# Second conditioning columns on ScalarE, output matrix at unit 13, state outputs and scores in pairs of 64 rows

## The chip, the core and the metric

The kernel runs on one core of one Trainium2 chip. The core has five engines that run side by side: TensorE (PE in the profile, its weight loads PEld), VectorE (DVE), ScalarE (ACT), GpSimd (POOL) and SyncE (SP, which here only issues transfers and takes branches). Each works through its own queue in order, and they wait for each other by semaphores. The metric is the device time of one execution in microseconds (us), lower is better.

## The reference

One layer of a diffusion backbone with 512 latent tokens and 256 context tokens of 1024 channels, all float32, cut to what matters here:

```python
mod = silu(c) @ ada_w + ada_b;  mod_c = silu(c_ctx) @ ada_w + ada_b
sh1, sc1, g1, sh2, sc2, g2 = split(mod, 6);  csh1, csc1, ... = split(mod_c, 6)
h  = rms_norm(x, norm_mix_w) * (1 + sc1) + sh1          # latent
hc = rms_norm(ctx, norm_mix_w) * (1 + csc1) + csh1      # context
p, pc = h @ w_in, hc @ w_in                             # q, k, v, r, low rank, u
gla = gated linear attention of q, k, v in chunks, both directions, times silu(r)
s5  = complex diagonal state space over u, both directions, then gelu and GLU
x = x + g1 * (concat([gla, s5]) @ w_out)
h2 = rms_norm(x, norm_ffn_w) * (1 + sc2) + sh2
x = x + g2 * moe(h2)             # the top 4 of 32 experts, clamped SwiGLU
return rms_norm(x, final_norm_w)
```

## The kernel before

The **prologue** (0 to about 480 us of the profile) computes everything up to the routing of h2. The **expert loop** after it streams the weights of all 32 experts (1 MB pieces gu and dn) and multiplies the tokens that were routed to each. The prologue is put in order by a scheduler, from the order of the code and priorities (`high_priority` moves work ahead), with stretches whose order on some engines is written by hand (`manual_schedule`).

**First stage.** The projection to u, the S5 inputs, is done in 32 units: four parts h of the 1024 input channels (256 each), times four 128-column tiles of the latent (`pu`, 512 columns wide) and of the context (`puc`, 256 wide). On TensorE and ScalarE their order is the loop `for i, (h, o)` (i from 4 to 31), into which other work is put at certain numbers i:

- `ADA1 = (7, 8, 9, 10)`: the shifts of the second half of the conditioning (`ps_ada`, L273). After the last, `columns(1)` makes the scale A1 and the shift B1 of channels 512 to 1023 for latent and context: the rows are copied from PSUM to `mrow` (L282), turned by two transposes into `ps_mod` (L115), and added to and multiplied by weight columns. Then `modulate(1)` (L555) applies them in eight activations to xn and xc. Parts h = 2 and 3 (units 16 to 31) need it.
- `LOW = 20`: the low rank gates. `OUT = 23`: `output_columns` turns the S5 output matrix in two runs of 32 small transposes (`ps_c`, L441), each copied to `cc` by ScalarE (L443). From `COND0 = 12` each unit also does a piece of the other conditioning product (`pa`, L527), whose weights `adb` come through SyncE. From `CHUNK0 = 14` each unit turns four blocks of chunk weights (`ps_w`), which VectorE makes at L428 to L430 (`wr`, `wi`, with `wtmp`) and ScalarE copies to `wt` (L422).

`work(...)` gives a buffer from one ring of four (tag t2k) that mrow, wtmp, bt, uT and others share. After unit 31 ScalarE copies pu to `uT`, SyncE sends it out (`ud`), and VectorE makes the products `cl` (L467 to L469, with wtmp again). Then TensorE computes q, k (`pk`), v and r, while VectorE scans the S5 states (`XV`) up to about 304 us.

**Second stage** (304 to 363 us). `space_out(j)` makes the S5 outputs py: for each of 16 pairs of groups, two products of `TZ` with U (64 columns each) and four of `xb` with cl. xb holds the states of two groups of 64 rows as block diagonals (128x128, zeros elsewhere), copied out of XV by ScalarE (first group, L997) and VectorE (second, L995). `attend(tp)` does the linear attention of two chunks: for each of two heads h2 of a pair (rows 0 to 63, rows 64 to 127) four score products `psc` (64 rows, L1047), masked into `pm_` by ScalarE and VectorE (L1052 to L1055), four products of states `po<-sm` (L1060) and two of values (L1062). A float32 product is two records in the profile.

**The join.** `gla_out` normalizes po to gl, whose transposes pgl start behind a branch on SyncE (`steep`, L1086); the output projection pmx follows. SyncE's queue ahead of that branch holds loads of x, `wo` and the first `gu`.

## Time and profile before

| | |
|---|---|
| time before, median of 3 runs | 1516.83 us (1516.59 to 1519.24) |
| the profiled execution | 1516.56 us |
| its span in the profile | 1514.7 us |
| TensorE busy over the span | 1345.6 us (89%) |
| VectorE, ScalarE, GpSimd busy | 529.8, 251.1 and 178.1 us |
| bytes moved by DMA | 487.19 MB, mean 322 GB/s |

The page of the profile divides the span into 40 slices and gives for each the busy share of every engine and of the 16 DMA engines. Other views give the busy time in a stretch, or an engine's instructions in the order of time: start, duration, line, operation, what is written from what, shapes, count, and in brackets the idle time ahead of it and what ended that. One line can stand for several records ("x4"), whose duration then runs from the first start to the last end. PEclk is the share of full speed (2.4 GHz) that TensorE's clock was granted.

### The profile page before, as it was taken

Reading aid. Unit: us, or ns where it says so; the run is one execution under the profiler, and the core shown is the slowest. Engines: PE = TensorE matmul, PEld = TensorE weight load, DVE = VectorE, ACT = ScalarE, POOL = GpSimd, SP = SyncE. Lnnn points to the kernel's source line nnn. Section 1 sums busy time; section 2 is a strip of 40 time slices with the busy share of each in tenths; the row PEclk is TensorE's granted clock in tenths of the full one; section 3 lists DMA queues with packets and bytes.
Section 4 is the critical chain, followed back from the end, with each engine's and each line's share of the span. In section 5 each row is a group of like instructions: output and inputs, shape, how many; then the busy total and the mean of one; then the engine's idle time right before and its main releaser. Section 6 shows DMA issues by size and latency. Waiting matters only on the chain. (4 is left out here: it accounts for less than half of the span.)

```text
span 1514.7 us, 21032 instructions
## 1 busy us (share of the span) xinstructions
PE 1345.6 (89%) x8123; PEld 544.4 (36%) x8123; DVE 529.8 (35%) x1373; ACT 251.1 (17%) x552; POOL 178.1 (12%) x158
## 2 busy tenths in 40 slices
PE   5679689997997899999998999999998988788985
PEld 2334354476443233333333333333332223222322
DVE  5941848966155221321122211222211132112125
ACT  4122351163121100100001000010000010000014
POOL 1030000000002010120102011111111111111110
PEclk9889799998997999999999999999999999999998
DMA  9565225134466999999999999999999999999993
GB/s 327 187 213 177 72 84 125 42 123 174 167 218 230 391 370 415 409 408 412 413 413 407 418 406 412 413 413 410 412 407 405 412 414 410 408 407 409 411 406 117
DMA packets 108428, 487.19 MB, mean 322 GB/s; under 512 B 25470, under 2 KB 32398, under 8 KB 59152
## 3 DMA queue, kind: packets, MB, share of 16 engines
q1 hardware_dynamic: 92704, 457.16, 75.8%
q0 software_dynamic: 13872, 24.72, 6.0%
q10 hardware_dynamic: 1728, 3.56, 0.6%
q8 instruction: 88, 1.44, 0.4%
q14 instruction: 36, 0.29, 0.1%
HBM read 468.41 MB, written 22.86 MB: 324 GB/s over the span
## 5 line engine op out<-in xcount | busy, mean ns | idle before, releaser
L1637 PE MATMUL pg<-gu,xT 128*64 128x512 f32 x2048 | 480.3, 601 | 35.2 <-DMA gu<-in_exp_w_gu_dram 28.6
L1637 PEld LDWEIGHTS pg<-gu,xT 128*64 128x64 f32 x2048 | 138.1, 137 | 331.4 <-issue 240.9
L1670 PE MATMUL pd<-dn,aT 128*64 128x512 f32 x992 | 222.8, 594 | 12.2 <-DMA dn<-in_exp_w_down_dram 9.6
L1657 DVE TENSOR_SCALAR at<-rest 128x256 f32<-128x256 f32 x32 | 13.6, 425 | 544.6 <-PE rest L1650 307.8
L1658 ACT ACTIVATE sgm<-at 128x256 f32<-128x256 f32 x96 | 39.7, 414 | 699.2 <-DVE at L1657 658.8
L1670 PEld LDWEIGHTS pd<-dn,aT 128*64 128x64 f32 x992 | 68.4, 136 | 145.8 <-issue 110.6
L1605 POOL DMA_INDIRECT xg<-h2d,iu x47 | 50.3, 1069 | 590.9 <-DVE li L1659 297.3
L1650 PE MATMUL rest<-gu,xT 128*32 128x512 f32 x896 | 107.3, 597 | 0.0
L1721 POOL DMA_INDIRECT acc<-y,iu x30 | 47.1, 1569 | 195.0 <-DMA acc<-yr,iu 165.7
L1621 ACT ACTIVATE aT<-turn 128x512 f32<-128x512 f32 x64 | 27.9, 487 | 204.8 <-PE turn L115 199.9
L1721 POOL DMA_INDIRECT acc<-yr,iu x30 | 48.1, 1604 | 63.1 <-DMA acc<-y,iu 40.0
L1719 DVE SCALAR_TENSOR_TENSOR yr<-rest,gt,g2r 128x256 f32<-128x256 f32 x30 | 14.5, 483 | 104.2 <-DMA acc<-yr,iu 71.6
L1680 PE MATMUL rest<-dn,aT 128*32 128x256 f32 x896 | 50.8, 379 | 0.0
L1650 PEld LDWEIGHTS rest<-gu,xT 128*32 128x32 f32 x896 | 24.4, 109 | 69.1 <-issue 67.9
L115 PE MATMUL turn<-ident,at 128*128 128x128 f32 x192 | 31.9, 302 | 9.4 <-PEq L1755 4.7
L1519 DVE CAST e<-mt 96x64 bf16<-96x64 f32 x32 | 6.1, 200 | 90.8 <-PEq L1755 46.8
L1661 DVE TENSOR_TENSOR at<-at,sgm 128x256 f32<-128x256 f32 x96 | 37.6, 419 | 0.0
L1660 DVE SCALAR_TENSOR_TENSOR at<-li,at 128x256 f32<-128x256 f32 x96 | 37.5, 418 | 0.0
L577 PE MATMUL pu<-xn,wu_w 128*128 128x512 f32 x64 | 35.7, 686 | 1.2 <-issue 1.2
L115 PEld LDWEIGHTS turn<-ident,at 128*128 128x128 f32 x192 | 25.8, 209 | 30.2 <-issue 25.9
L1567 DVE TENSOR_TENSOR ohs<-mt 128x1024 bf16<-128x1024 f32 x30 | 36.5, 1216 | 0.0
L115 PE MATMUL turn<-ident,xg 128*128 128x128 f32 x192 | 28.1, 284 | 6.9 <-PEq L1746 5.5
(554 smaller groups left out, 1434.2 us busy)
## 6 DMA issues: line engine op xcount, KB each, us to landing
gu<-in_exp_w_gu_dram SPq DMA_DIRECT2D x252, 1024.0 KB
dn<-in_exp_w_down_dram SPq DMA_DIRECT2D x128, 1024.0 KB
adb<-in_ada_w_dram SPq DMA_DIRECT2D x32, 512.0 KB
ada<-in_ada_w_dram SPq DMA_DIRECT2D x16, 512.0 KB
wo<-in_w_out_dram SPq DMA_DIRECT2D x4, 1024.0 KB
gu<-in_exp_w_gu_dram POOLq DMA_DIRECT2D x4, 1024.0 KB, 8.4
xt<-in_x_dram SPq DMA_DIRECT2D x4, 512.0 KB
wu_w<-in_w_in_dram SPq DMA_DIRECT2D x4, 512.0 KB
```

The lines of the kernel that those rows point to most:

```text
L115: nc.tensor.transpose(ps, src, ident[:k, :k])
L577: nc.tensor.matmul(o, lhs(k, w[:, kk]), rhs(k, w[:, kk]), start=opens and k == 0, stop=k == KT - 1, skip_group_check=True)
L1567: V.tensor_tensor(ohs, iot.rearrange("p (o s) r -> p o (s r)", o=1).to_broadcast([P, 4, 2 * P]), pm.to_broadcast([P, 4, 2 * P]), op=OP.is_ ...
L1605: last = nc.gpsimd.indirect_dma_start(out=x[:, c0:c1], out_offset=None, in_=src, in_offset=bass.IndirectOffsetOnAxis(ap=iu[:, s:s + 1], ax ...
L1637: nc.tensor.matmul(pg[b][64 * q:64 * q + 64], xT[:, k % 4, (k // 4) * 64:(k // 4 + 1) * 64], gu[k][:, :, c:c + 256], start=False, stop=(k ...
L1650: nc.tensor.matmul(pr[32 * q:32 * q + 32], xT[:, 4 + k % 2, (k // 2) * 32:(k // 2 + 1) * 32], gu[k][:, :, q * 256:(q + 1) * 256], start=Fa ...
L1658: nc.scalar.activation(sg, at, AF.Sigmoid, scale=1.702)
L1660: V.scalar_tensor_tensor(at, li, 1.0, at, op0=OP.add, op1=OP.mult)
L1661: V.tensor_tensor(at, at, sg, op=OP.mult)
L1670: nc.tensor.matmul(pd[64 * q:64 * q + 64], aT[:, k % 4, (k // 4) * 64:(k // 4 + 1) * 64], dn[k][:, q * 512:(q + 1) * 512], start=False, st ...
L1680: nc.tensor.matmul(pe[32 * q:32 * q + 32, 0:256], aT[:, 4 + k % 2, (k // 2) * 32:(k // 2 + 1) * 32], dn[k][:, q * 256:(q + 1) * 256], star ...
L1721: nc.gpsimd.indirect_dma_start(out=dst, out_offset=bass.IndirectOffsetOnAxis(ap=iu[:, s:s + 1], axis=0), in_=src, in_offset=None, bounds_c ...
```

## The change

It has six parts. (1) `mrow` of the second conditioning half gets a buffer of its own. (2) Its A1 and B1 are made by eight ScalarE activations of 128x2 straight from PSUM, with bias and scale from columns; the copy `pms` and the six GpSimd operations go. `one_more` now holds (1 + b) w. The first half stays on VectorE. (3) `OUT` goes from 23 to 13, `COND0` from 12 to 11 and `CHUNK0` from 14 to 12. (4) Two edge fills of kc2 move from VectorE to GpSimd. (5) `space_out` reads the states from XV: each block diagonal product becomes two of 64 rows and 64 columns, one per group, next to each other, on rows and columns 0 to 63 and 64 to 127. xb, its copies and its zero fills go. (6) `attend` issues the score products and the products of states of both heads in turn, ahead of the masks; each head has its own PSUM bank for scores.

```diff
-OUT = 23
-COND0 = 12
-CHUNK0 = 14
+OUT = 13
+COND0 = 11
+CHUNK0 = 12
...
-            mrow = work("mrow", (P, 256))
+            mrow = consts.tile([P, 256], F32, name="mrow1") if p else work("mrow", (P, 256))
...
-            if p:
-                pms = consts.tile([P, 256], F32, name="pms")
-                nc.scalar.activation(pms, pm[:, :256], AF.Copy)
-                pm = pms
...
+            if p:
+                for kk in range(4):
+                    a, b, w = [o[:, n + 4 * p + kk:n + 4 * p + kk + 1] for o, n in ((one_more, 0), (cols, 16), (cols, 32))]
+                    nc.scalar.activation(A1[p][:, :, kk], pmv[:, 1, kk // 2, kk % 2, 0:2], AF.Identity, bias=a, scale=w)
+                    nc.scalar.activation(B1[p][:, :, kk], pmv[:, 0, kk // 2, kk % 2, 0:2], AF.Identity, bias=b)
+                return
...
-                eng.tensor_tensor(a_, pmv[:, 1, :, :, j], one_more[:, p].rearrange("p (h b) -> p h b", h=2), op=OP.add)
-                eng.tensor_tensor(a_, a_, col(32), op=OP.mult)
-                eng.tensor_tensor(b_, pmv[:, 0, :, :, j], col(16), op=OP.add)
+                V.scalar_tensor_tensor(a_, pmv[:, 1, :, :, j], 1.0, col(24), op0=OP.add, op1=OP.add)
+                V.tensor_tensor(a_, a_, col(32), op=OP.mult)
+                V.tensor_tensor(b_, pmv[:, 0, :, :, j], col(16), op=OP.add)
...
-    V.memset(kc2[:, 0, :, LC - 1:LC], 0.0)
-    V.memset(kc2[:, 1, :, 0:1], 0.0)
+    nc.gpsimd.memset(kc2[:, 0, :, LC - 1:LC], 0.0)
+    nc.gpsimd.memset(kc2[:, 1, :, 0:1], 0.0)
...
-                        nc.tensor.matmul(o, x[:, i % 2, d * 2 + r].rearrange("p g w -> p (g w)"),
-                                         cl[j][r][:, d, gl_].rearrange("p k c -> p (k c)"),
-                                         start=False, stop=(d == 1 and r == 1), skip_group_check=True)
+                        for g2 in range(2):
+                            xh = XV[g2 * 64:(g2 + 1) * 64]
+                            src = bass.AP(tensor=xh.tensor, offset=xh.offset + gp * 260 + d * 131 + r * 65,
+                                          ap=[list(xh.ap[0]), [1, 64]])
+                            nc.tensor.matmul(o[g2 * 64:(g2 + 1) * 64], src,
+                                             cl[j][r][g2 * 64:(g2 + 1) * 64, d, gl_].rearrange("p k c -> p (k c)"),
+                                             start=False, stop=(d == 1 and r == 1), skip_group_check=True)
...
+            pb = [bank("psc").rearrange("p (z h t) -> p z h t", z=2, h=2) for h2 in range(2)]
...
+            for z in range(2):
+                for hp in range(2):
+                    for h2 in range(2):
+                        nc.tensor.matmul(pb[h2][:, z, hp], kd[z][hs[h2], hp, c * P:(c + 1) * P],
+                                         qd[z][hs[h2], hp, c * P:(c + 1) * P], start=True, stop=True)
```

What the scheduler makes of it is shown at three places. First TensorE behind the second conditioning half, before (`ps_ada` are the shifts, `wu_w` the weights of the units, `adb` those of the conditioning):

```order
L273 MATMUL ps_ada_604<-ada_157,stc 32x256 x8
L115 MATMUL ps_mod<-ident,mrow 128x128 x2
L577 MATMUL puc_197<-xc,wu_w_146 128x256 x2
L577 MATMUL pu_195<-xn_108,wu_w_146 128x512 x2
L527 MATMUL pa_735<-adb_199,stc 32x512 x4
L577 MATMUL puc_198<-xc,wu_w_146 128x256 x2
L527 MATMUL pa_735<-adb_199,stc 32x512 x4
L577 MATMUL pu_196<-xn_108,wu_w_146 128x512 x2
```

and after:

```order
L273 MATMUL ps_ada_604<-ada_157,stc 32x256 x8
L115 MATMUL ps_mod<-ident,mrow_645 128x128 x2
L578 MATMUL puc_197<-xc,wu_w_146 128x256 x2
L528 MATMUL pa_733<-adb_199,stc 32x512 x4
L578 MATMUL pu_195<-xn_108,wu_w_146 128x512 x2
L528 MATMUL pa_733<-adb_199,stc 32x512 x4
L115 MATMUL ps_w<-ident,wr_558 128x128 x4
L578 MATMUL puc_198<-xc,wu_w_146 128x256 x2
L442 MATMUL ps_c_756<-ident,crow_105 64x32 x32
L442 MATMUL ps_c_790<-ident,crow_106 64x32 x32
```

The first chunk weights (ps_w) now stand two units earlier, and the output matrix (ps_c) ten. On ScalarE at the same place before:

```order
L282 ACTIVATE mrow<-ps_ada_604 128x256
L290 ACTIVATE pms<-ps_mod 128x256
L555 ACTIVATE xn_109<-xn_109,B_653,A_652 128x512
L555 ACTIVATE xc<-xc,B_653,A_652 128x256
L555 ACTIVATE xn_109<-xn_109,B_653,A_652 128x512
```

and after (A and B are the scale and shift columns):

```order
L281 ACTIVATE mrow_645<-ps_ada_604 128x256
L293 ACTIVATE A_650<-ps_mod,one_more,cols 128x2
L294 ACTIVATE B_651<-ps_mod,cols 128x2
L293 ACTIVATE A_650<-ps_mod,one_more,cols 128x2
L294 ACTIVATE B_651<-ps_mod,cols 128x2
```

Two more pairs of A and B follow there before the modulations, which are the same eight. The third place is TensorE at the first state outputs, before (pst, pkt and pp belong to the attention states):

```order
L999 MATMUL py<-TZ_1859,U_1074 64x128
L999 MATMUL py<-TZ_1859,U_1075 64x128
L999 MATMUL py<-TZ_1859,U_1074 64x128
L999 MATMUL py<-TZ_1859,U_1075 64x128
L936 MATMUL pst<-vc,kt__2017 64x128 x8
L115 MATMUL pkt_2051<-ident,cum_1269 128x128 x4
```

and after:

```order
L983 MATMUL py<-TZ_1859,U_1074 64x128
L983 MATMUL py<-TZ_1859,U_1075 64x128
L992 MATMUL py<-cl_1110,XV 64x128 x2
L992 MATMUL py<-cl_1111,XV 64x128 x2
L992 MATMUL py<-cl_1110,XV 64x128 x2
L992 MATMUL py<-cl_1111,XV 64x128 x2
L983 MATMUL py<-TZ_1859,U_1074 64x128
L983 MATMUL py<-TZ_1859,U_1075 64x128
L992 MATMUL py<-cl_1110,XV 64x128 x2
L992 MATMUL py<-cl_1111,XV 64x128
L937 MATMUL pst<-vc,kt__2017 64x128 x16
L115 MATMUL pkt_2051<-ident,cum_1269 128x128 x4
```

The products with cl no longer wait for copies of XV and stand ahead of the attention states; each x2 is a pair of row halves.

## Rows read from the trace of the kernel before

**Rows 1.** the page's forty slices: busy tenths of the DMA engines

```profile
DMA  9565225134466999999999999999999999999993
```

**Rows 2.** busy time by stretch: columns engine busy (instructions), PEclk, DMA share, GB/s

```profile
70.00:80.00 10.00, 2.56 (x7) 2.17 (x8) 10.00 (x18) 0.77 (x2) 1.37 (x1) 0.50 0.00 2
130.00:140.00 10.00, 10.00 (x58) 4.33 (x56) 3.06 (x5) 2.39 (x4) 0.00 (x0) 0.71 0.40 134
315.00:363.00 48.00, 48.00 (x367) 38.97 (x364) 29.54 (x85) 25.84 (x62) 3.82 (x14) 1.00 0.33 109
640.00:680.00 40.00, 39.38 (x230) 13.02 (x228) 11.71 (x34) 5.15 (x13) 9.50 (x7) 1.00 1.02 408
```

**Rows 3.** order of time, TensorE, 61 to 103: start, us, idle before, releaser

```profile
62.93 1.07 PE L273 MATMUL ps_ada<-ada,stc 128*32 128x256 f32 x16
77.44 0.69 PE L115 MATMUL ps_mod<-ident,mrow 128*128 128x128 f32 x2 [13.43 <-ACT mrow L282]
...
79.62 2.69 PE L577 MATMUL pu<-xn,wu_w 128*128 128x512 f32 x4
...
85.30 1.98 PE L577 MATMUL pu<-xn,wu_w 128*128 128x512 f32 x4
...
98.02 1.11 PE L115 MATMUL ps_w<-ident,wi 128*128 128x128 f32 x4 [7.29 <-ACT wt L422]
98.93 3.27 PE L577 MATMUL pu<-xn,wu_w 128*128 128x512 f32 x4
```

**Rows 4.** order of time, ScalarE, 61 to 105 and at 363

```profile
77.00 0.38 ACT L282 ACTIVATE mrow<-ps_ada 128x256 f32<-128x256 f32 x1 [17.29 <-DVE wr L430]
...
92.59 0.81 ACT L555 ACTIVATE xn<-xn,B,A 128x512 f32<-128x512 f32 x1 [14.05 <-POOL A L302]
...
97.39 0.57 ACT L422 ACTIVATE wt<-ps_w 128x512 f32<-128x512 f32 x1
...
363.11 0.20 ACT L1935 ACTIVATE rt<-ms 128x4 f32<-128x4 f32 x1
```

**Rows 5.** order of time, GpSimd, 61 to 105

```profile
78.63 13.33 POOL L301 TENSOR_TENSOR A<-pms,one_more 128x4 f32<-128x4 f32 x1 [72.97 <-ACT pms L290]
91.93 0.18 POOL L303 TENSOR_TENSOR B<-pms,cols 128x4 f32<-128x4 f32 x1
```

**Rows 6.** order of time, TensorE, 125 to 136

```profile
128.08 2.88 PE L441 MATMUL ps_c<-ident,crow 32*64 32x32 f32 x64 [0.69 <-ACT cc L443]
```

**Rows 7.** order of time, VectorE, 120 to 182

```profile
160.16 2.50 DVE L468 TENSOR_TENSOR wtmp<-cc,pw 128x512 f32<-128x512 f32 x4 [1.66 <-DMA ud<-uT]
...
175.81 1.30 DVE L469 TENSOR_TENSOR cl<-cl,wtmp 128x512 f32<-128x512 f32 x2
```

**Rows 8.** order of time, TensorE, at 182

```profile
181.79 4.56 PE L577 MATMUL pk<-xn,wqk_w 128*128 128x512 f32 x10
```

**Rows 9.** order of time, TensorE, 347.7 to 350.8: state outputs

```profile
347.84 0.44 PE L999 MATMUL py<-TZ,U 128*64 128x128 f32 x4
348.20 1.16 PE L1003 MATMUL py<-cl,xb 128*128 128x128 f32 x8
349.29 0.44 PE L999 MATMUL py<-TZ,U 128*64 128x128 f32 x4
```

**Rows 10.** order of time, TensorE, 316 to 317 and 355 to 357: scores

```profile
316.74 0.27 PE L1060 MATMUL po<-sm,qd 64*128 64x128 f32 x1
316.85 0.27 PE L1047 MATMUL psc<-qd,cum 64*128 64x128 f32 x1
316.86 0.27 PE L1060 MATMUL po<-sm,qd 64*128 64x128 f32 x1
...
355.57 0.71 PE L1060 MATMUL po<-sm,qd 64*128 64x128 f32 x4
356.21 0.49 PE L1062 MATMUL po<-vv,pm__2399 128*128 128x128 f32 x2
```

**Rows 11.** order of time, ScalarE, at 375

```profile
374.79 1.15 ACT L1015 ACTIVATE y<-ys 128x512 f32<-128x512 f32 x2 [9.03 <-SPq L1086]
```

More of the change, by code (lines that the diff above doesn't have):

```diff
@@ L276, in columns @@
     def columns(p):
-        eng = nc.gpsimd if p else V
         with tc.high_priority():
-            mrow = work("mrow", (P, 256))
+            mrow = consts.tile([P, 256], F32, name="mrow1") if p else work("mrow", (P, 256))
             if p:
@@ L603, in hybrid_layer_kernel @@
     todo_c = [(g, k) for g in range(2) for k in range(KT)]
-    one_more = consts.tile([P, 2, 4], F32, name="one_more")
+    one_more = consts.tile([P, KT], F32, name="one_more")
     with tc.manual_schedule(engines={mybir.EngineType.PE, mybir.EngineType.Activation}):
@@ L611, in hybrid_layer_kernel @@
         silu()
-        V.tensor_scalar(one_more.rearrange("p a b -> p (a b)"), cols[:, 24:32], 1.0, None, OP.add)
+        V.scalar_tensor_tensor(one_more, cols[:, 24:32], 1.0, cols[:, 32:40], op0=OP.add, op1=OP.mult)
         decays()
@@ L973, in hybrid_layer_kernel @@
     ys = place(1, "ys", (P, 8, 256))
-    xb = [whalf(f"xb{i}", (P, 2, 4, 2, 64)) for i in range(2)]
-    for t in xb:
-        nc.gpsimd.memset(t, 0.0)
     def space_out(j):
@@ L984, in space_out @@
                 gp = j * 8 + gl_
-                x = xb[gl_ // 2 % 2]
                 o = py[:, i * P:(i + 1) * P]
-                if i % 2 == 0:
-                    for g2 in range(2):
-                        xh = XV[g2 * 64:(g2 + 1) * 64]
-                        for n in range(2):
-                            src = bass.AP(tensor=xh.tensor, offset=xh.offset + (gp + n) * 260,
-                                          ap=[list(xh.ap[0]), [131, 2], [65, 2], [1, 64]])
-                            dst = x[g2 * 64:(g2 + 1) * 64, n, :, g2].rearrange("p (d r) w -> p d r w", d=2)
-                            if g2:
-                                V.tensor_copy(dst, src)
-                            else:
-                                nc.scalar.activation(dst, src, AF.Copy)
                 for g2 in range(2):
@@ L1041, in attend @@
             c = tp * 2 + ti
-            for h2 in range(2):
-                hs = slice(h2 * 64, (h2 + 1) * 64)
-                pb = bank("psc").rearrange("p (z h t) -> p z h t", z=2, h=2)
-                for z in range(2):
-                    for hp in range(2):
-                        nc.tensor.matmul(pb[:, z, hp], kd[z][hs, hp, c * P:(c + 1) * P],
-                                         qd[z][hs, hp, c * P:(c + 1) * P], start=True, stop=True)
+            hs = [slice(h2 * 64, (h2 + 1) * 64) for h2 in range(2)]
@@ new lines, in attend @@
+            pb = [bank("psc").rearrange("p (z h t) -> p z h t", z=2, h=2) for h2 in range(2)]
[4 more added lines that the diff above has]
+                                         qd[z][hs[h2], hp, c * P:(c + 1) * P], start=True, stop=True)
+            for hp in range(2):
+                for z in range(2):
+                    for h2 in range(2):
+                        nc.tensor.matmul(po[h2][:, (ti * 2 + hp) * P:(ti * 2 + hp + 1) * P], qd[z][hs[h2], hp, c * P:(c + 1) * P],
+                                         sm[z][hs[h2], hp, c], start=(ti == hp == z == 0), stop=False, skip_group_check=True)
@@ L1050, in attend @@
+            for h2 in range(2):
                 pm_ = work("pm_", (P, 2, P))
                 fw = work("fw", (P, 2, P))
-                nc.scalar.activation(fw, pb[:, 0], AF.Copy)
-                V.tensor_tensor(pm_, fw, pb[:, 1], op=OP.add)
+                nc.scalar.activation(fw, pb[h2][:, 0], AF.Copy)
+                V.tensor_tensor(pm_, fw, pb[h2][:, 1], op=OP.add)
                 V.copy_predicated(pm_, keep[:, 0:1].to_broadcast([P, 2, P]), fw)
-                V.copy_predicated(pm_, keep[:, 1:2].to_broadcast([P, 2, P]), pb[:, 1])
+                V.copy_predicated(pm_, keep[:, 1:2].to_broadcast([P, 2, P]), pb[h2][:, 1])
@@ L1056, in attend @@
                 for hp in range(2):
-                    o = po[h2][:, (ti * 2 + hp) * P:(ti * 2 + hp + 1) * P]
                     h = hp * 2 + h2
-                    for z in range(2):
-                        nc.tensor.matmul(o, qd[z][hs, hp, c * P:(c + 1) * P], sm[z][hs, hp, c],
-                                         start=(z == 0), stop=False, skip_group_check=True)
-                    nc.tensor.matmul(o, pm_[:, hp], vv[:, c, h * P:(h + 1) * P],
+                    nc.tensor.matmul(po[h2][:, (ti * 2 + hp) * P:(ti * 2 + hp + 1) * P], pm_[:, hp], vv[:, c, h * P:(h + 1) * P],
```

## The prediction

> **What bounds the kernel now.** I read the slices of the span first, then busy time by stretch, then the order of time on each engine. The slices [rows 1] show two halves: from the fourteenth (about 492 us) on the DMA engines are full, at 9 tenths or more, and inside the expert loop they stay at a share of 1.02 and 408 GB/s [rows 2]. That loop streams a fixed set of expert weights and begins only after routing (in the two slices ahead the share is 6 tenths), and this change leaves its order alone. So I take its length as fixed and ask only when it starts: whatever ends the prologue earlier ends the kernel earlier, one for one.
>
> In the prologue two stretches are touched. The first is the projection of the S5 inputs, where TensorE follows an order written by hand. It ends the second conditioning's shifts at 62.93 + 1.07 = 64.00 and does nothing until the transposes of mrow at 77.44, 13.43 of it put down to mrow on ScalarE; it stands idle again for 7.29 before 98.02 [rows 3]. The second is 315 to 363 us, where TensorE is busy 48.00 of 48.00, VectorE 29.54 and ScalarE 25.84 [rows 2]: what is taken off TensorE counts there, what is taken off the other two does not.
>
> **First hole.** ScalarE's copy to mrow starts at 77.00 after 17.29 idle, and its releaser is VectorE's wr, not TensorE [rows 4]. The data was ready at 64.00; what was missing is a slot of the four-slot work ring, held by VectorE's chunk weights. With a buffer of its own the copy starts at about 64.0, and the transposes follow 0.4 later (77.00 to 77.44), so TensorE goes on 13.0 earlier.
>
> **Second hole.** GpSimd's first add starts at 78.63 and takes 13.33, while the next of the same shape takes 0.18 [rows 5]. ScalarE, in order, waits for these adds until 92.59, then does eight modulations, and only at 97.39 the copy wt that releases TensorE [rows 4]. In the new kernel eight activations of 128x2 straight from PSUM stand where the copy pms and the six adds were. Such an activation is not in the trace; the nearest row is one of 128x4 with 0.20 [rows 4], so eight cost 0.8 (if they overlap by half) to 1.6 (end to end), and if each paid the 0.57 of the wide wt row 4.6. I take 1.6, by the nearest row. After an mrow at 64.0 and the transposes they end near 67, and the modulations (92.59 to 97.39 = 4.8) near 72. Up to there TensorE has units 11 to 15, conditioning products and now the output matrix's transposes, which even without that matrix lasted from 77.44 to 98.02 - 7.29 = 90.7 [rows 3]. So the 7.29 go, even at 4.6.
>
> **Slow clock.** Behind each hole the same product is longer: pu 2.69 at 79.62 and 3.27 at 98.93, against 1.98 at 85.30 [rows 3]; the granted clock in 70 to 80 is 0.50, that is 1.2 GHz [rows 2]. Without the holes 0.71 + 1.29 = 2.0 come back, a lower bound, since more than pu falls into the slow time.
>
> **What takes their place.** CHUNK0, two units earlier, asks at unit 12, near 70, for weights that VectorE still works on: up to 1 us. The output matrix's second run of transposes waits for ScalarE's cc, 0.69 before [rows 6], and cc now stands behind modulations: again up to 1. TensorE queues everything behind these waits, so I charge 0.5 each. The runs themselves cost the same at unit 13 as at 23. Sum: 13.0 + 7.3 + 2.0 - 1.0 = 21.3 us, with a little for the other slow matmuls **21.5**.
>
> **Does it reach the end of the prologue?** After unit 31 VectorE finishes the cl products. They stop once, for the transfer ud<-uT until 160.16, and end at 175.81 + 1.30 = 177.1 [rows 7]; TensorE starts pk at 181.79 [rows 8]. The stop hangs on uT, the outputs of the last units, and so moves by the gain. What follows is the same chain, so all up to 304 shifts with it. A limit is DMA: the conditioning weights now have to come within some 20 us less. In 70 to 80 the DMA share was 0.00 [rows 2], so there is room to fetch earlier, but buffers come free only as TensorE uses them. I leave 18 to 25 for the stage.
>
> **State outputs.** Per group pair TensorE does four TZ records and eight of block diagonals; the next begins 349.29 - 347.84 = 1.45 later, and the eight take 349.29 - 348.20 = 1.09 of it [rows 9]. There are 16. The new form has sixteen records of 64 rows and 64 columns, two by two on different halves of rows and columns. If a pair runs together, that is eight steps again, and nothing is saved. If not, it is eight more steps: at most +1.09 x 16 = +17.4. Row halves do run together in the trace: a psc at 316.85 and a po at 316.86 start 10 ns apart, 0.11 after the po of 316.74 [rows 10]. Those write different banks of PSUM; here both halves write py, in other partitions of one bank. I take together, with +1 for pairs that the scheduler splits. The removed copies on ScalarE and VectorE and the two zero fills on GpSimd lay beside a full TensorE: 0.
>
> The Trainium skill speaks against this piece: TensorEngine Tiling, Restrictions and Gotchas, Gotcha 1, says that different row tiles cannot access the same PSUM bank simultaneously. By it the pairs go one after the other, which is rival A below. No row here shows row halves in one bank.
>
> **Scores.** There are 64 psc and 64 po<-sm records. Four po without a partner take 356.21 - 355.57 = 0.64 [rows 10], 0.16 each; a psc costs between a step of 0.11 and that. So they cost 10.2 + 7.0 to 10.2 = 17.2 to 20.4 now. In pairs at 0.11 they are 64 steps = 7.0. Each change of form costs at most 1.09 - 8 x 0.11 = 0.2 [rows 9]; at 16 to 24 changes that takes 3 to 5 back. The gain is 5 to 10; if no pair forms it is 0, or a loss of 3 by the changes. I take 6, and with the 1 lost above **5**. VectorE's part of the scores is unchanged and must not come late; it has 48.00 - 29.54 = 18 us to spare there.
>
> **Join.** Behind the last scores the program joins at a branch: ScalarE's y starts at 374.79 after 9.03 idle, released by SyncE [rows 11]. SyncE's loads of x, wo and gu now stand in another order ahead of that branch, and VectorE has a product that reads nfw, a transfer, in front of its last gl. Either may move the end by -3 to +3; I take -1.5. The kc fills that move to GpSimd find it idle: 0.
>
> **Sum.** -21.5 - 5 - 1.5 = -28, from 1516.56 (the span of 1514.7 and 1.9 around it; the median 1516.83 is 0.3 higher): **1488.5**.
>
> **Rivals.** A: the 64-row pairs in one bank run one after the other: +14 by steps of 0.11, +17.4 at most, so about 1504. For it: no row shows the form. Against it: the four TZ records, column halves of one bank, take 348.20 - 347.84 = 0.36, less than four steps of 0.11 [rows 9], so one bank alone forbids nothing. B: the first stage is fed too slowly, by conditioning weights or VectorE's chunk weights, and only the first hole's 13 survive: 1516.56 - 13 - 6.5 = 1497. For it: all DMA of that stretch waits for TensorE to free buffers; against it: the idle queue of 70 to 80. C, on the other side: TensorE's clock. In 130 to 140, behind the run of 32-row transposes from 128.08 [rows 6], it was 0.71 with TensorE busy throughout [rows 2]. If the narrow products of 315 to 363 bring it to 0.50, the 43 us left there take 86: 1488.5 + 43 = 1532. It decides from a mean clock of 0.61 (43 / 0.61 - 43 = 28). Against it: before, 128 narrow records lay in that stretch at a clock of 1.00 [rows 2]. D: the expert loop is not tied to the prologue and nothing changes: 1516.5. Against it: a share of 6 tenths ahead of it [rows 1] and full from there.
>
> **How the numbers follow.** Forecast 0.64; A 0.15; B 0.12; C 0.05; D 0.04. The likeliest case runs from 1516.56 - 25 - 11 - 3 = 1477.5 to 1516.56 - 18 - 5 + 3 = 1496.5. Eight in ten need B and half of A: 1477 to 1503. Faster by over 0.2% (3 us, about what a measurement of this kernel can tell from no change): 0.91, within 0.2%: 0.04, slower: 0.05.
>
> **What would show it.** The copy mrow within 1 us of the last ps_ada; no TensorE wait over 1 us from there to unit 31; cl ended near 155.5, pk from about 160. In the later stretch two py records reading XV within 10 ns of each other and the next pair 0.11 later (in A all stand 0.11 apart), a clock of 1.00, and some 5 us less from the first TZ to the last score. The prediction is wrong if the expert loop does not start as much earlier as pk does, or if the first stage gives under 15.

## The result

The changed kernel takes 1483.43 us (median of 4 runs, 1481.54 to 1486.64), against 1517.1 for the kernel before on the same occasions: a ratio of 0.9778, 95% interval [0.9758, 0.9797], or 33.7 us less. The forecast was 1488.5, in a range of 1477 to 1503. The profiled execution has a span of 1481.3, 33.4 less than before.

The line of its page with the busy tenths of the DMA engines, which answers to [rows 1]; the slices are 37 us wide now:

```profile
DMA  9765133156359999999999999999999999999992
```

The full slices begin one earlier (the thirteenth, about 444 us). Where the 33.4 us went is read from eight marks that both traces have: the ends of the last ps_ada and of unit 31 (the last puc), the first pk, the first pkt of kc, the end of the last py or po, the first pmx, the first pg of the expert loop, and the end of the span. Length of each stretch in us, of the two kernels and of five of the experiments told below:

| stretch up to | before | changed | e3 | e4 | e5 | e6 | e8 |
|---|---|---|---|---|---|---|---|
| last ps_ada ended | 64.0 | 65.2 | 67.0 | 64.1 | 62.9 | 67.5 | 65.1 |
| unit 31 ended | 91.1 | 67.4 | 67.1 | 67.3 | 90.5 | 90.4 | 65.1 |
| first pk | 26.7 | 28.2 | 26.7 | 29.1 | 27.2 | 27.1 | 15.1 |
| first pkt of kc | 121.8 | 122.5 | 125.3 | 124.7 | 121.8 | 121.7 | 117.7 |
| last py or po ended | 59.3 | 50.5 | 58.2 | 58.2 | 57.4 | 50.6 | 50.5 |
| first pmx | 13.6 | 11.1 | 13.7 | 13.4 | 13.7 | 13.5 | 11.3 |
| first pg<-gu | 99.0 | 96.0 | 99.0 | 98.5 | 99.0 | 97.8 | 96.6 |
| end of the span | 1039.2 | 1040.4 | 1039.1 | 1040.5 | 1041.1 | 1038.8 | 1039.7 |

The last line is the expert loop with what follows it: 1038.8 to 1041.1 in all seven (1038.5 to 1041.1 in all fourteen profiles), whatever the prologue does. Before to changed, the lines add to +1.2 - 23.7 + 1.5 + 0.7 - 8.8 - 2.5 - 3.0 + 1.2 = -33.4.

**The first stage.** TensorE of the changed kernel, order of time, 60 to 105 us; it answers to [rows 3]:

```profile
64.17 1.07 PE L273 MATMUL ps_ada<-ada,stc 128*32 128x256 f32 x16
65.74 0.44 PE L115 MATMUL ps_mod<-ident,mrow 128*128 128x128 f32 x2 [0.51 <-ACT mrow L281]
...
72.83 0.63 PE L115 MATMUL ps_w<-ident,wr 128*128 128x128 f32 x4 [1.88 <-DVE wr L431]
...
77.00 2.60 PE L442 MATMUL ps_c<-ident,crow 32*64 32x32 f32 x64 [0.70 <-ACT cc L444]
...
82.31 3.27 PE L578 MATMUL pu<-xn,wu_w 128*128 128x512 f32 x4
```

The 13.43 are down to 0.51, and the 7.29 are gone. New is a wait of 1.88 for the chunk weights at unit 12. The 0.70 between the runs of the output matrix stood there before too (0.69 [rows 6]), and so did a slow pu behind them (2.97 at 133.66; 3.27 now, at a granted clock of 0.50 in 80 to 85, that is 1.2 GHz). From the last ps_ada to the end of unit 31, TensorE is idle for 22.14 us before and for 3.80 now, and busy for 68.95 and 63.55, at a mean granted clock of 0.85 and 0.95. ScalarE at the same place, which answers to [rows 4]:

```profile
65.30 0.38 ACT L281 ACTIVATE mrow<-ps_ada 128x256 f32<-128x256 f32 x1 [3.63 <-PE ps_ada L273]
66.22 0.35 ACT L293 ACTIVATE A<-ps_mod,one_more,cols 128x2 f32<-128x2 f32 x1 [0.53 <-PE ps_mod L115]
...
67.76 0.85 ACT L556 ACTIVATE xn<-xn,B,A 128x512 f32<-128x512 f32 x1
```

The copy mrow starts 0.06 after the last ps_ada ended (64.17 + 1.07). Of the eight small activations the first starts at 66.22, and the first modulation follows them at 67.76. VectorE in order of time, 105 to 180 us, which answers to [rows 7]: its first wtmp of the cl products that waits, and the last cl, which ends at 154.05 + 1.28 = 155.3 (177.1 before):

```profile
134.96 0.69 DVE L469 TENSOR_TENSOR wtmp<-cc,pw 128x512 f32<-128x512 f32 x1 [3.94 <-ACT uTc L694]
...
154.05 1.28 DVE L470 TENSOR_TENSOR cl<-cl,wtmp 128x512 f32<-128x512 f32 x2
```

TensorE's first pk in the same order of time, which answers to [rows 8]:

```profile
160.80 5.42 PE L578 MATMUL pk<-xn,wqk_w 128*128 128x512 f32 x12
```

**The second stage.** TensorE's busy time from the first pkt of kc to the last score, by the view of busy time by stretch (columns as in [rows 2]), in the kernel before:

```profile
303.62:362.88 59.26, 57.02 (x479) 46.37 (x478) 37.94 (x99) 32.74 (x79) 5.81 (x17) 1.00 0.34 112
```

and in the changed one:

```profile
283.32:333.77 50.45, 50.21 (x603) 40.41 (x602) 28.15 (x73) 28.01 (x63) 2.20 (x4) 1.00 0.47 156
```

TensorE had 59.26 - 57.02 = 2.24 us idle there before and has 0.24 now, at a clock of 1.00 both times. The view of groups by line, TensorE, same stretch, in the kernel before (columns: busy us, mean ns of one, idle before; groups overlap by their tails, so they are compared one by one and not added up to the stretch), and under it the busy time by stretch of one line alone, the products of the values (columns: length, busy time of PE and of PEld with their counts, clock, DMA):

```profile
L1003 PE MATMUL py<-cl,xb 128*128 128x128 f32 x128 | 19.3, 290 | 0.0
L1060 PE MATMUL po<-sm,qd 64*128 64x128 f32 x64 | 11.5, 297 | 0.0
L1047 PE MATMUL psc<-qd,cum 64*128 64x128 f32 x64 | 8.5, 286 | 0.0
L999 PE MATMUL py<-TZ,U 128*64 128x128 f32 x64 | 7.2, 296 | 0.0
```

```profile
303.62:362.88 59.26, 7.51 (x32) 4.77 (x32) 1.00 0.34 112
```

The same two views of the changed kernel:

```profile
L992 PE MATMUL py<-cl,XV 64*64 64x128 f32 x256 | 20.4, 278 | 0.0
L983 PE MATMUL py<-TZ,U 128*64 128x128 f32 x64 | 7.8, 297 | 0.0
L1037 PE MATMUL psc<-qd,cum 64*128 64x128 f32 x64 | 7.3, 290 | 0.2 <-DVE sqo L1020 0.2
L1042 PE MATMUL po<-sm,qd 64*128 64x128 f32 x64 | 6.2, 282 | 0.0
```

```profile
283.32:333.77 50.45, 5.43 (x32) 4.09 (x32) 1.00 0.47 156
```

Scores and products of states went from 11.5 + 8.5 = 20.0 to 7.3 + 6.2 = 13.5, products of values from 7.5 to 5.4; state outputs went from 19.3 + 7.2 = 26.5 up to 20.4 + 7.8 = 28.2. TensorE in order of time, rows that answer to [rows 9] and [rows 10]:

```profile
299.96 1.16 PE L1037 MATMUL psc<-qd,cum 64*128 64x128 f32 x16
300.95 0.39 PE L1042 MATMUL po<-sm,qd 64*128 64x128 f32 x4
...
315.05 1.09 PE L992 MATMUL py<-cl,XV 64*64 64x128 f32 x16
316.07 0.44 PE L983 MATMUL py<-TZ,U 128*64 128x128 f32 x4
```

Sixteen psc take 0.99 to the next instruction, 0.062 each, and sixteen py of 64 rows 1.02 up to the next TZ (eight block diagonals took 1.09). The two py of a pair start 0.007 apart and the next two 0.11 later. Not every record has a partner. Of the 64 psc and 64 po<-sm records, 24 start within 0.02 us of another of them before and 84 now, and of the 256 py of 64 rows 228 do; a run without partners is that of eight psc from 303.02, which stand 0.11 apart.

### The profile page after: what moved, and what is told of

It reads as the page before. It is cut to its first block, busy times and chain, and to the rows that moved or that the text cites. A ratio compares the mean times of both kernels' runs of the same rounds, so it can differ in the third digit from the quotient of the medians.

```text
span 1481.3 us, 21251 instructions
## 1 busy us (share of the span) xinstructions
PE 1335.3 (90%) x8251; PEld 536.6 (36%) x8251; DVE 523.9 (35%) x1355; ACT 247.3 (17%) x543; POOL 162.2 (11%) x152
## 5 line engine op out<-in xcount | busy, mean ns | idle before, releaser
L1649 DVE TENSOR_SCALAR at<-rest 128x256 f32<-128x256 f32 x32 | 13.6, 425 | 561.5 <-PE rest L1642 310.7
```

## The experiments

The ratios are against the kernel before, timed on the same chip in the same rounds; a difference in us that is worked out from ratios is theirs times 1517. The kernel before took 1517.1 on the occasion of the result and 1519.1, 1519.2 and 1520.3 on those of the experiments, so times in us of different occasions are not compared with each other.

### Is it the buffer, the engine or the numbers?

e1: the kernel before with the buffer alone (the copy pms reuses it, for want of room).

```diff
-            mrow = work("mrow", (P, 256))
+            mrow = consts.tile([P, 256], F32, name="mrow1") if p else work("mrow", (P, 256))
...
-                pms = consts.tile([P, 256], F32, name="pms")
+                pms = mrow
```

> The kernel before, with a buffer of its own for mrow of the second half (pms then uses the same buffer); GpSimd still does the six adds. Theory: GpSimd's first add is not slow in itself but held up until VectorE's run of 128x512 two-input operations is over (91.96 against 91.8 before), so mrow starts near 64.5, the add starts near 66 and then lasts some 26 us, TensorE's first hole is gone and the second grows to about 20: time within 3 us of before. Rival: the add takes its 13.3 us wherever it starts, ends near 79, and the first hole's 13 us are saved: about 1504 us.

Measured: 0.9969 [0.9948, 0.9990], about 4.7 us less, neither of the two. TensorE in order of time, 60 to 105 us:

```profile
68.02 0.44 PE L115 MATMUL ps_mod<-ident,mrow 128*128 128x128 f32 x2 [0.51 <-ACT mrow L282]
...
92.06 1.11 PE L115 MATMUL ps_w<-ident,wi 128*128 128x128 f32 x4 [12.61 <-ACT wt L422]
```

The first hole is gone and the second grew from 7.29 to 12.61. GpSimd in the same order of time:

```profile
69.72 10.33 POOL L303 TENSOR_TENSOR B<-mrow,cols 128x4 f32<-128x4 f32 x1
80.01 0.19 POOL L301 TENSOR_TENSOR A<-mrow,one_more 128x4 f32<-128x4 f32 x1
80.15 2.59 POOL L303 TENSOR_TENSOR B<-mrow,cols 128x4 f32<-128x4 f32 x1
82.69 4.05 POOL L302 TENSOR_TENSOR A<-A,cols 128x4 f32<-128x4 f32 x2
```

VectorE there; of its 128x32 operations, which stand between runs of wide ones, three:

```profile
79.88 0.22 DVE L324 TENSOR_TENSOR ctmp<-lv 128x32 f32<-128x32 f32 x1
...
82.57 0.21 DVE L325 TENSOR_TENSOR lv<-lv,ctmp 128x32 f32<-128x32 f32 x1
...
86.45 0.18 DVE L321 TENSOR_TENSOR ctmp<-lv 128x32 f32<-128x32 f32 x1
```

GpSimd gets on where VectorE does something narrow: its long B ends at 69.72 + 10.33 = 80.05, just behind VectorE's narrow op of 79.88, the next long one at 82.74 behind that of 82.57, the last at 86.74 behind that of 86.45. In between it stands for 10.33, 2.59 and (two together) 4.05 us, with operations of which one takes 0.19 at 80.01. So it is held up by VectorE's wide operations, as theory said, but it gets in at some of their gaps. Not at each: a narrow operation of VectorE at 75.96 went by while GpSimd stood, and in the kernel before the add that starts at 78.63 [rows 5] stood through those at 82.49, 85.10 and 89.05 and ended at 91.96. Ten runs of e1 lie between 1507.29 and 1519.57, wider apart than those of any other kernel here; that they differ by the gap that GpSimd catches is likely, but only one of them has a trace. The Trainium skill (SBUF — State Buffer, Who interferes with whom) calls the ports that VectorE and GpSimd share an exclusive lock, and GPSIMD Engine Reference, Specifications, names VectorE instructions with two SBUF inputs among those that contend. These rows agree: VectorE's wide operations here are such. The narrow ones are tensor_tensor operations too, so what lets GpSimd in beside them these rows don't show.

e2: the activations without the buffer.

```diff
-                pms = consts.tile([P, 256], F32, name="pms")
-                nc.scalar.activation(pms, pm[:, :256], AF.Copy)
-                pm = pms
...
+                for kk in range(4):
...
+                    nc.scalar.activation(A1[p][:, :, kk], pmv[:, 1, kk // 2, kk % 2, 0:2], AF.Identity, bias=a, scale=w)
+                    nc.scalar.activation(B1[p][:, :, kk], pmv[:, 0, kk // 2, kk % 2, 0:2], AF.Identity, bias=b)
```

> The kernel before, with the second half's columns made by the eight ScalarE activations, but mrow still in the shared ring. Theory: the first hole of 13.4 us stays (mrow starts near 77, released by VectorE's wr), the second of 7.3 goes together with about 1.3 of slow clock behind it: 8.6 us less, about 1508. Rival: both holes hang on the buffer alone, the activations bring nothing: 1517.

Measured: 0.9937 [0.9913, 0.9962], 9.6 us less. ScalarE's copy is still late, but the wt that follows the modulations now waits for TensorE and no longer the other way round. ScalarE in order of time, 62 to 100 us:

```profile
79.41 0.38 ACT L281 ACTIVATE mrow<-ps_ada 128x256 f32<-128x256 f32 x1 [17.29 <-DVE wr L431]
...
91.09 0.60 ACT L423 ACTIVATE wt<-ps_w 128x512 f32<-128x512 f32 x1 [4.06 <-PE ps_w L115]
```

e3: both, and nothing else; to the diff of e2 comes

```diff
-            mrow = work("mrow", (P, 256))
+            mrow = consts.tile([P, 256], F32, name="mrow1") if p else work("mrow", (P, 256))
```

> The kernel before with both: own buffer and ScalarE activations, units and everything else as before. Theory: both holes go; TensorE's pk starts 21 to 23 us earlier and the time is 1494 to 1496. If the two parts simply added up, the sum of e1 and e2 would be about 9; theory says that together they give more than twice that.

Measured: 0.9861 [0.9842, 0.9879], 21.1 us less; more than 4.7 + 9.6 = 14.3, because with the buffer alone the second wait takes up 12.61 - 7.29 = 5.3 of what was freed. The stretch to unit 31 is 67.1, about as in the changed kernel. TensorE has the order of the kernel before up to pk here, so the gain can be parted: it is idle for 1.92 instead of 22.14 up to the end of unit 31, and busy for 65.20 instead of 68.95, at a mean granted clock of 0.95 instead of 0.85. So 20.2 us are the waits and 3.75 the clock. 3.4 us are given back up to the first pkt of kc (125.3 against 121.8).

e4: e3 with the new numbers, OUT 13, COND0 11, CHUNK0 12. And e11: the changed kernel with the old three, as this diff of it against the changed kernel shows.

```diff
-OUT = 13
-COND0 = 11
-CHUNK0 = 12
+OUT = 23
+COND0 = 12
+CHUNK0 = 14
```

> As e3_columns, with OUT 13, COND0 11 and CHUNK0 12, so the whole first stage of the change. Theory: against e3 nothing, within 1 us (the holes are gone already; 1.9 us of waiting for wr at unit 12 and slow products behind the output matrix against 2 units of lead for the chunk weights). Rival: the new numbers carry part of the gain, because the last ps_w releases VectorE's cl earlier: 3 to 6 us less than e3.

> The changed kernel with OUT 23, COND0 12 and CHUNK0 14 as before. Theory, from e3 against e4: the new numbers carry 0 to 2 us, so 1483.5 to 1485.5. Rival: they cost, by the 1.88 us that TensorE waits for wr at unit 12 and the slow products behind the output matrix: 1481 to 1483.

Measured: e4 0.9843 [0.9826, 0.9861] against e3's 0.9861, and e11 0.9772 [0.9754, 0.9790] against the changed kernel's 0.9778. Both pairs overlap, and they point in opposite ways. In the traces the way from the last ps_ada to pk takes 93.8 in e3 and 93.9 in e11, with the old numbers, and with the new ones 96.4 in e4, 95.6 in the changed kernel and 93.3 to 93.4 in e7, e9 and e12, which have the same order on TensorE and ScalarE up to pk. So single profiles of one order differ here by 3 us, and no cost of the new numbers shows either. That part of the change is worth nothing that can be measured.

### Which half of the second stage?

e5: the kernel before with the new state outputs alone. e6: with the new scores alone. The core of e5's edit:

```diff
-                        nc.tensor.matmul(o, x[:, i % 2, d * 2 + r].rearrange("p g w -> p (g w)"),
-                                         cl[j][r][:, d, gl_].rearrange("p k c -> p (k c)"),
...
+                        for g2 in range(2):
...
+                            nc.tensor.matmul(o[g2 * 64:(g2 + 1) * 64], src,
+                                             cl[j][r][g2 * 64:(g2 + 1) * 64, d, gl_].rearrange("p k c -> p (k c)"),
```

And of e6's:

```diff
-            for h2 in range(2):
...
-                for z in range(2):
-                    for hp in range(2):
-                        nc.tensor.matmul(pb[:, z, hp], kd[z][hs, hp, c * P:(c + 1) * P],
...
+            for z in range(2):
+                for hp in range(2):
+                    for h2 in range(2):
+                        nc.tensor.matmul(pb[h2][:, z, hp], kd[z][hs[h2], hp, c * P:(c + 1) * P],
```

> The kernel before with the state outputs alone in the new form (pairs of 64 rows from XV, no block diagonals). Theory: a pair costs one step, so 16 x (1.39 - 1.45) = 1 us less on TensorE; besides, TensorE's waits between 303.6 and 315 (1.18, 0.67 and 0.25 in the profile before, and some slack at VectorE and ScalarE) are filled, since the first products need no copies any more: together 2 to 5 us less, 1512 to 1515. Rival: the pairs gain nothing in the whole and only the scores do: within 1 us of before.

> The kernel before with the scores alone in the new order (row halves in turn, all eight score products and eight state products ahead of the masks). Theory: 128 records at 0.065 instead of 0.09 to 0.16 each save 5 to 8 us on a full TensorE: 1509 to 1512. Rival: the masks on VectorE come late and take it back: 0 to 2 us less.

Measured: e5 0.9984 [0.9968, 0.9999], 2.4 us less; e6 0.9916 [0.9895, 0.9936], 12.8 less, more than theory gave. In the stretch itself e5 saves 1.9, e6 8.7, and both together 8.8, so they do not add: on top of the scores the new state outputs bring nothing there. Their groups cost 1.7 us more on TensorE (26.5 to 28.2); by its busy time in the stretch it is 0.2 in e5 (57.02 to 57.22) and 1.8 on top of e6 (48.39 to 50.20). What they bring is the 2 us of idle time that they fill, since they stand ready without copies. The columns (e3, 21.1) and the scores (e6, 12.8) add up to 33.9, as much as the whole change (33.7); a kernel with these two alone was not tried. TensorE's groups by line in e6, in the stretch of the table:

```profile
L1053 PE MATMUL po<-sm,qd 64*128 64x128 f32 x64 | 6.7, 283 | 0.0
L1048 PE MATMUL psc<-qd,cum 64*128 64x128 f32 x64 | 6.0, 293 | 0.0
```

Scores and products of states fall to 6.0 + 6.7 = 12.7 there, from 20.0; 102 of their 128 records start within 0.02 us of another.

e7: the changed kernel with the four products of one row half ahead of the four of the other.

```diff
-                for d in range(2):
-                    for r in range(2):
-                        for g2 in range(2):
-                            xh = XV[g2 * 64:(g2 + 1) * 64]
+                for g2 in range(2):
+                    xh = XV[g2 * 64:(g2 + 1) * 64]
+                    for d in range(2):
+                        for r in range(2):
```

> The changed kernel with the same 64-row products of the state outputs, but all four of one row half before the four of the other, so that no two neighbours are on different halves, except at the turn. Theory: the halves run together only when they stand next to each other; eight records of one half take 8 x 0.11 each: 16 x 0.8 = 11 to 14 us more on TensorE, 1494 to 1498. Rival: TensorE looks far enough ahead to pair them anyway, or the stage is not bound by TensorE: within 3 us of 1483.

Measured: 0.9797 [0.9778, 0.9816], beside 0.9778 for the changed kernel: 0.0019 or 2.9 us more, inside the intervals, and by its number the rival. The trace shows more. TensorE in order of time, one group pair and the TZ behind it:

```profile
318.19 1.58 PE L992 MATMUL py<-cl,XV 64*64 64x128 f32 x16
319.70 0.44 PE L983 MATMUL py<-TZ,U 128*64 128x128 f32 x4
```

Busy time of the stretch up to the last py or po:

```profile
280.67:338.29 57.62, 57.62 (x603) 47.16 (x602) 29.32 (x80) 28.62 (x65) 2.20 (x4) 1.00 0.45 147
```

Sixteen records take 1.51 to the next TZ instead of 1.02, and the stretch is 57.62 instead of 50.45. So the pairs do run together in the changed kernel, and one bank is no hindrance. But unpaired cost only 0.49 each time, not the 0.8 expected: with sixteen single steps of 0.11 it would be 1.76, so part of the second half still ran beside the first, though four instructions away (its first record starts at 318.684, beside one of the first half at 318.678). Of the 7.2 us in the stretch less is seen in the time: the join is 9.7 here (11.1 in the changed kernel), and this profile's start is 1.1 earlier.

e12: the changed kernel's scores in the same lots, but head by head.

```diff
-            for z in range(2):
-                for hp in range(2):
-                    for h2 in range(2):
+            for h2 in range(2):
+                for z in range(2):
+                    for hp in range(2):
                         nc.tensor.matmul(pb[h2][:, z, hp], ...
...
-            for hp in range(2):
-                for z in range(2):
-                    for h2 in range(2):
+            for h2 in range(2):
+                for hp in range(2):
+                    for z in range(2):
                         nc.tensor.matmul(po[h2][:, ...
```

> The changed kernel with the scores issued in the same lots ahead of the masks, but head by head, so that neighbours are mostly on the same row half. Theory: the scores' gain of 8.7 us in e6 is part pairing, part fewer changes of form; without pairs each of the 128 records costs 0.095 to 0.11 instead of 0.065 to 0.07, which is 3 to 5 us on TensorE: 1486 to 1489. Rival: it is all grouping, pairs bring nothing: within 1 us of 1483.4.

Measured: 0.9772 [0.9753, 0.9790], no difference to the changed kernel. Its two groups by line on TensorE, in the stretch that answers (284.91 to 336.12):

```profile
L1037 PE MATMUL psc<-qd,cum 64*128 64x128 f32 x64 | 8.1, 288 | 0.0
L1042 PE MATMUL po<-sm,qd 64*128 64x128 f32 x64 | 7.9, 288 | 0.0
```

8.1 + 7.9 = 16.0, against 20.0 before and 13.5 in the changed kernel: of the 6.5 us, 4.0 are left in this order. It doesn't part grouping from pairs cleanly, since 54 of the 128 records still start within 0.02 us of another here (24 before, 84 in the changed kernel). The stretch is 51.2, only 0.8 longer; the state outputs fell out 0.6 cheaper in this order (20.2 + 7.4), and TensorE's last 0.24 of idle time are gone.

### The join

In the kernel before the DMA engines are full until just ahead of the join and then idle. Its busy time by stretch there (columns as in [rows 2]; y starts at 374.79 [rows 11]):

```profile
370.00:372.70 2.70, 2.70 (x15) 2.60 (x13) 0.00 (x0) 0.00 (x0) 0.00 (x0) 0.50 0.94 370
372.70:375.00 2.30, 0.30 (x2) 0.00 (x0) 0.00 (x0) 0.21 (x1) 0.00 (x0) 0.50 0.08 34
```

No packet moves in the last 0.62 us ahead of y (DMA share 0.00 in 374.17 to 374.79). VectorE's last gl ended at 369.01, 5.8 ahead of y. TensorE there:

```profile
369.35 3.65 PE L115 MATMUL pgl<-ident,gl 128*128 128x128 f32 x16 [2.78 <-DVEq L1086]
...
376.47 2.07 PE L1145 MATMUL pmx<-wo,glT 128*128 128x512 f32 x2 [3.47 <-ACT glT L1162]
```

So the pgl do not start behind SyncE's branch, as the description of the join has it, but 0.34 behind the last gl. What the branch holds is ScalarE's y, and with it the copy glT that pmx waits for. In e1 to e6, which have the join of the kernel before, the last packet ends 0.57 to 0.64 ahead of y as well. In the changed kernel SyncE issues the four loads of x between 323.25 and 328.6, well ahead of the last score; before, two of them stood behind wo and gu, at 362.27. VectorE in order of time ahead of the branch:

```profile
340.78 0.69 DVE L1023 TENSOR_TENSOR gl<-sqo,rw 128x512 f32<-128x512 f32 x1
```

ScalarE's y behind it, and TensorE:

```profile
342.71 1.15 ACT L1004 ACTIVATE y<-ys 128x512 f32<-128x512 f32 x2 [7.25 <-PE pgl L115]
```

```profile
341.81 3.25 PE L115 MATMUL pgl<-ident,gl 128*128 128x128 f32 x16 [1.65 <-DVEq L1078]
344.90 13.90 PE L1137 MATMUL pmx<-wo,glT 128*128 128x512 f32 x32
```

The last gl ends at 340.78 + 0.69 = 341.47, the pgl follow 0.34 later, y 1.2 later, and pmx follows the pgl without a wait: VectorE bounds it in this profile. The last gl comes 7.7 behind the last score here and came 6.1 behind it before; ahead of it stands VectorE's product with nfw, 1.22 us from 338.53.

e9: the four loads of x behind the branch.

```diff
-    nc.sync.dma_start(R["bparts"][:, 2 * D:], bias[1])
+    R["bl"] = nc.sync.dma_start(R["bparts"][:, 2 * D:], bias[1])
...
-        nc.sync.dma_start(x1[t], I["x"][0, t * P:(t + 1) * P])
+        with tc.issue_after(R["bl"].ins):
+            nc.sync.dma_start(x1[t], I["x"][0, t * P:(t + 1) * P])
```

> The changed kernel with the four loads of x (2 MB) behind the branch of the join instead of ahead of it. Theory: SyncE gets past the branch only when the loads it issued ahead have landed; that is why the join comes 11.1 us after the last score here and 13.6 before, and with 2 MB less it is bound by VectorE's last gl, about 8 us after: 1 to 3 us less, 1480.5 to 1482.5. Rival: the join waits for VectorE alone, or the bytes are owed later anyway: within 0.5 us of 1483.4.

Measured: 0.9756 [0.9739, 0.9772], beside 0.9778 [0.9758, 0.9797]: 3.3 us less, with intervals that overlap, so the time alone decides nothing. The trace does: y comes 0.36 behind the last gl instead of 1.2, but the join is 11.5 long, with pmx again right behind the pgl. That is the rival: in the changed kernel's profile VectorE bounds pmx already. This is not so in each run: in e12, whose join has the same code, y comes 4.5 behind the last gl, released by SyncE, pmx waits 1.44 for glT, and the join takes 13.2. That the loads bounded it before is read from the traces of seven kernels; it was not tried on the kernel before.

### What is late next

e8: the second term of the cl products in eight slots of a space that is free then, not in the ring.

```diff
+        cds, n_ = keep_.tile([P, 8, 512], F32, name="cds", tag="xv"), [0]
...
-                        cd = work("wtmp", (P, 4, 8, 16))
+                        cd = cds[:, n_[0] % 8].rearrange("p (g k c) -> p g k c", k=8, c=16)
+                        n_[0] += 1
```

> The changed kernel with the second term of the cl products (wtmp) in eight slots of the space that the conditioning weights leave free, instead of the shared ring. In the changed kernel VectorE waits 3.94 and 0.44 us there for uT and ud, and ScalarE's gates wait 20.59 for cl, both by that ring. Theory: cl ends 4 us earlier and the gates' activations, which keep ScalarE busy from 155 to 175, start at once behind unit 31: pk and what follows move by 4 to 12 us, 1471 to 1479. Rival: TensorE's pk comes behind plag whatever ScalarE does: only the 4 us, or nothing.

Measured: 0.9643 [0.9626, 0.9660], 1464.72 us: 0.0135 or 20.5 us less than the changed kernel, and beyond what theory gave. ScalarE in order of time, the first gate activation of the changed kernel:

```profile
154.82 0.69 ACT L751 ACTIVATE ab<-pg,cols 128x512 f32<-128x512 f32 x1 [20.59 <-DVE cl L470]
```

The same in e8:

```profile
137.01 0.69 ACT L753 ACTIVATE ab<-pg,cols 128x512 f32<-128x512 f32 x1 [5.26 <-DMA ud<-uT]
```

VectorE's last cl in e8:

```profile
135.69 4.90 DVE L472 TENSOR_TENSOR cl<-cl,cds 128x512 f32<-128x512 f32 x8
```

The ring that held mrow up in the kernel before still held up two things in the changed one: VectorE's wtmp, for more than the 3.94 put down to ScalarE's uTc, and ScalarE's gates for 20.59, put down to VectorE's cl. Neither is new. In the kernel before, ScalarE's first gate activation stands like this:

```profile
176.59 0.69 ACT L750 ACTIVATE ab<-pg,cols 128x512 f32<-128x512 f32 x1 [19.85 <-DVE cl L469]
```

With other slots VectorE makes its second terms from 116.42 on instead of 134.96, ahead of the end of unit 31, and cl ends at 135.69 + 4.90 = 140.6, 14.7 earlier. The gates start at 137.01, and pk at 145.21: the stretch from unit 31 to pk is 15.1 instead of 28.2, and the next stretch gains 4.9 more (117.7 against 122.5). Whether pk follows cl or the gates this run can't tell, since both came earlier: pk starts 4.6 behind the last cl here, 5.5 in the changed kernel and 4.7 before.

e10: e8 and e9 together.

> e8_ring and e9_join together. Theory: they lie in different stages, so their gains add: e8's 1464.7 less what e9 gains, 1462 to 1464. Rival: the earlier prologue meets the same loads, nothing is added: 1465.

Measured: 0.9635 [0.9618, 0.9652], 1465.8 us, as e8: e9 adds nothing to it.

## Why the prediction was right, point by point

- **The end moves with the prologue, one for one.** Right: the last line of the table. Rival D (nothing changes) is out.
- **First hole, 13.0.** Right in mechanism and size (13.43 down to 0.51): mrow was waiting for a slot. e2, which keeps the ring, keeps ScalarE's 17.29 ahead of mrow; e1 and the changed kernel, with the buffer, have TensorE wait 0.51.
- **Second hole, 7.3.** Right. The eight activations cost 67.76 - 66.22 = 1.54 (1.6 forecast, by the nearest row). Both holes together were forecast at 20.3, and e3 measures 20.2.
- **Slow clock, 2.0.** Right in kind, and under-sized, as the prediction's words "a lower bound" allow: e3, with TensorE's order of before, is busy 3.75 less. Only the two pu were counted. One slow pu of 3.27 is left, behind the run of 32-row transposes, where one of 2.97 stood before.
- **What takes their place, 1.0.** Under-sized: 1.88 for the chunk weights; the 0.70 for cc is not new. 1.5 more went between unit 31 and pk, where gates' products now stand that stood ahead of unit 31 before. The new numbers of parts of the order were costed at waits only and brought nothing back (e4, e11). In sum the stage gave 21.0 at pk (181.79 - 160.80), forecast 21.5. That it is so near is partly luck: the clock gave 1.75 more than forecast and the wait took 0.9 more, and the last ps_ada ended 1.2 later, which is within what profiles of one order differ by. Rival B, with only 13, is out.
- **From pk to kc, 0.** Forecast to shift as a whole; it gave 0.7 back. TensorE is busy for 117.89 there before, at a mean granted clock of 0.99, and for 116.85 now, at 1.00; its idle time grew from 3.94 to 5.67.
- **State outputs, +1.** Nearly right in the price, 1.7 by groups, and wrong in leaving out what they fill: the 2.2 us of idle ahead of 315 us, since the stretch was read from 315 on, where TensorE was full, and not from 304. Rival A (one after the other in one bank) is out by e7 and by 1.02 for sixteen records. The rule of the Trainium skill that the prediction cited for it (TensorEngine Tiling (Array Packing), Restrictions and Gotchas, Gotcha 1) does not hold for these pairs: the measurement decides.
- **Scores, 6.** The term was mis-sized: 8.7 in e6. Scores and states alone gave 6.5 to 7.3. Another 2.1 came from a group that the prediction did not cost, the products of values (7.51 to 5.43): four of them stand together now, where they stood in twos before ([rows 10] has one such two). That pairs alone make the gain was not so: a third of the 128 records stand without a partner, and e12, with 54 that have one instead of 84, keeps 4.0 of the 6.5. The bound of 11 us in the range for the second stage has no working; the terms as they stand give 10 at most, less what the state outputs take.
- **Join, -1.5 (-3 to +3).** It came to -2.5, with the bound moved from SyncE to VectorE. The term was a guess inside its range, and that it came so is partly luck: with the same code the join is 9.7 in e7 and 13.2 in e12. Another 3.0 up to the expert loop were not forecast. TensorE's clock there is 0.50 (1.2 GHz) in 375 to 380 before, behind 365 to 375, in which it was busy for 4.74, and 1.00 (2.4 GHz) in 345 to 350 now, behind 335 to 345, with 5.86. Over the stretch TensorE is busy for 85.9 before, at a mean granted clock of 0.88, and for 82.3 now, at 0.93; its idle time hardly differs (13.2 and 13.7). All eight profiles with the new scores have 96.0 to 98.2 there and all six without them 98.5 to 99.6, so part of it seems to go with the scores; by which path is not shown.
- **Rival C** (half the clock in the second stage): out, 1.00 throughout.
- **The signs.** mrow came 0.06 behind the last ps_ada, cl ended at 155.3, pk started at 160.80, the py came in pairs and the clock was 1.00, as said. Two signs did not come: TensorE does wait over 1 us ahead of unit 31 (1.88), and from the first TZ to the last score it is 8.8 less and not some 5 (304.59 to 362.88 before, 284.29 to 333.77 now).

So the 5.4 us by which the forecast was too small (28 against 33.4 of the span) lie in the second stage (+3.8) and behind it (+4.0); the first stage gave 0.5 less, the way from pk to kc 0.7 less and the stretch from the expert loop on 1.2 less.

The 3.4 us that e3 gives back between pk and kc, and the 2.9 of e4, are of the same two kinds as the changed kernel's 0.7. TensorE is idle there for 5.35 in e3 and 6.20 in e4 (3.94 before, 5.67 in the changed kernel), and busy for 119.92 at a mean granted clock of 0.97 and for 118.48 at 0.99 (117.89 before, 116.85 in the changed kernel).

What stays open: what the kernel before would do at the join with fewer transfers ahead of it (not tried); how much of the scores' gain is grouping and how much pairs; what set pk earlier in e8, cl or the gates. The move of the kc fills was not tried by itself.

## What to carry to other kernels

- When an engine waits for an instruction that was ready long ago, look for the buffer, and for everybody else in its ring. The same ring of four slots cost 13 us in one place, which the change found, and 20 in another (e8), which stood in the trace before as well and was passed over: 19.85 us of idle time "released" by an engine that has nothing to do with the data.
- Two waits in a row on one path are worth less one by one (4.7 and 9.6) than together (21). Neither should be judged alone.
- Compare stretches between marks and not only totals, and let a stretch begin where the work begins and not where the engine is full.

## What was not expected of the hardware

- Products on different halves of rows and columns run together though they write one bank: sixteen in 1.02 us. And a half that stands four instructions later still overlaps in part: 1.51, not 1.76.
- A GpSimd operation of 128x4 that takes 0.18 beside narrow operations of VectorE took up to 13.33 [rows 5] beside wide two-input ones, and got in at some of the gaps between them. The ten times of e1 lie within 12 us.
- The kernel before, e5 and e6 have the same order of work up to unit 31, and in their profiles the last ps_ada ends at 64.0, 62.9 and 67.5. Such a difference of 4.6 us between single runs is as large as several of the effects in question.
